# Input projection of a hybrid Fourier and attention step, twelve pairs of channel blocks by one level of Strassen's recursion

## The chip, the cores and the metric

One core of a Trainium2 chip runs the whole step. The metric is the device time of one execution in microseconds (us), median over runs. The engines run beside each other, each through its own instruction queue in order: TensorE (PE, matrix products; its weight loads are PEld), VectorE (DVE), ScalarE (ACT), GpSimd (POOL) and SyncE (SP, which issues DMA transfers; POOL and ACT issue some too). Waits between engines are semaphores.

## What is computed

One layer on 1024 latent and 128 context tokens of 1024 channels, in float32. Cut to what matters here:

```python
h = rms_norm(x) * (1 + scale) + shift
u_f, z_f, cq, ckv, k_rope, z_a, g_f, g_a = split(h @ w_in)   # 512 512 256 128 32 512 1024 1024
y_f = (fourier_mix(u_f) * silu(z_f)) @ w_f_out
y_a = (attention(cq, ckv, k_rope) * silu(z_a)) @ w_a_out
merged = sigmoid(g_f) * y_f + sigmoid(g_a) * y_a
x = x + gate * (merged @ w_out)                              # then a final norm
```

Fourier mixing is linear, so `u_f` is never formed: its weights are transformed and folded into the first part. What this change concerns is the rest of the input projection: `z_f`, `z_a`, `g_f`, `g_a` (3072 channels, 24 blocks of 128) and the low-rank part `cq, ckv, k_rope` (416 channels).

## The kernel before

Channels lie on the 128 partitions, tokens along the columns. Every float32 operand is kept as two parts, a high one rounded to PE's format and a low rest, and `mm3` makes one product from three matmuls: high by high, low by high, high by low. `hi_pool` rounds on POOL and `lo_dve` makes the rest on DVE; `split` does both for a loaded tile.

The first part loads tokens, normalises, transposes and modulates them into `hTh`/`hTl` (8 tiles of 128 channels x 1152 tokens, high and low), and mixes folded positions through the Fourier weights (order written out in `SEQ`). The mixing's last matmul starts at 89.14 us of the profiled span. Then, in the order of the program:

- Fourier gates: `load_in` brings a block of 128 channels of `w_in` (512 KB) and splits it; `proj(w, c)` multiplies it with one of three chunks of `CH` = 384 tokens, 8 tiles x 3 matmuls. `gated` applies ACT's sigmoid and DVE's product. Four blocks, `zf`.
- The position transform (matrices loaded by `load_r` on POOL's queue, products L125 to L129 on `dft` tiles and L566, L567), whose results are combined and multiplied with `zf` into `fz`.
- 8 blocks of `g_a` by `merge_gate`, stored to DRAM; 8 blocks of `g_f`, each with the Fourier output map (`w_f_out`, 12 matmuls a chunk) and DVE's product L679.
- The low-rank part: `low_mm` (9 token tiles x 24 matmuls of 416 columns, norms and rotation) and `low_tr` (transposes; per tile ACT copies and DVE differences), set between blocks of `merge_gate`.
- 4 blocks of `z_a` by `gated`, with the first keys, queries and values between them; then the attention, the output map with the merge, and the output projection, none of which the change edits.

That makes 72 chunks x 24 = 1728 matmuls of 128 x 384 by `proj`.

The engines' instruction orders come from a scheduler that reorders the program by estimates. SBUF tiles of up to 4.6 KB a partition come from one pool of `NU` = 40 buffers (`U`), PSUM from 8 banks (`MM`): a load or a product waits until a buffer's last reader is done.

Of the kernel before, what the change touches and what calls it, by code (L numbers as in the profile page):

```python
# [64 lines left out]
def kernel(ctx: ExitStack, tc: tile.TileContext, a: dict):  # L65
# [56 lines left out]
    tail = [None]  # L122

    def mm3(out, lh, ll, rh, rl, start, stop, after=False):
        i = pe.matmul(out, lh, rh, start=start, stop=False)  # L125
# [2 lines left out]
        pe.matmul(out, lh, rl, start=False, stop=False)  # L128
        tail[0] = pe.matmul(out, ll, rh, start=False, stop=stop)  # L129
# [318 lines left out]
    def load_in(i):
        return split_w(a["w_in"][i], [P, 8, P])

    def proj(w, c):
        wh, wl = w
        ps = MM()
        sl = slice(c * CH, (c + 1) * CH)
        for k in range(8):
            mm3(ps[:, :CH], wh[:, k, :], wl[:, k, :], hTh[k][:, sl], hTl[k][:, sl], k == 0, k == 7)
        return ps

    def gated(w, out, hook=None):
        for c in range(3):  # L460
            ps = proj(w, c)
            s = H([P, CH], s="sz")
            act.activation(s, ps[:, :CH], AF.Sigmoid)
            dve.tensor_tensor(out=out[:, c * CH : (c + 1) * CH], in0=ps[:, :CH], in1=s, op=ALU.mult)
            if hook:
                hook(c)

# [16 lines left out]
    pool.memset(zer, 0.0)
# [1 line left out]
    pool.memset(ex, 0.0)
# [49 lines left out]
    zf = []  # L536
    ahead = []
    for m in range(4):
        w = wn
        wn = load_in((1, 2, 3, 16)[m])  # L540
        if m == 3:
            ahead.append(load_in(17))
        z = U([P, NT], F32, "zf")
        gated(w, z)
        zf.append(z)
        if m == 0:
            freq512()
        if m == 2:
            ch, cl, sh, sl_ = [load_r(a["pos"][i], [P, 2, 512]) for i in range(4)]
# [31 lines left out]
    fz = []  # L581
    for p in range(2):
        qs = slice(p * P, (p + 1) * P)
        ss = slice(256 + p * P, 256 + (p + 1) * P)
# [6 lines left out]
        Ev, Fv = U([P, 640], F32, "E"), U([P, 640], F32, "F")
        dve.tensor_tensor(out=pairs(Ev[:, 0:512]), in0=pairs(A[:, 0:512]), in1=freqs(pb), op=ALU.subtract)
        dve.tensor_tensor(out=pairs(Fv[:, 0:512]), in0=pairs(A[:, 0:512]), in1=freqs(pb), op=ALU.add)
        dve.tensor_tensor(out=Ev[:, 512:640], in0=A[:, 512:640], in1=pc[:, 128:256], op=ALU.subtract)
        dve.tensor_tensor(out=Fv[:, 512:640], in0=A[:, 512:640], in1=pc[:, 128:256], op=ALU.add)
        for r in range(2):
            f = U([P, NT], F32, "f")
            z = zf[2 * p + r]
            if r == 0:
                x0, x1 = Ev, Fv  # L600
            else:
                x0, x1 = Fv, Ev
                for i in range(2):
                    g = 2 * p + i
                    act.copy(Fv[64 * i : 64 * i + 1, :], a64[32 * g : 32 * g + 1, :])
# [709 lines left out]
```

## Time and profile before

| | us |
|---|---|
| median of 3 runs | 957.46 |
| lowest and highest of them | 956.80, 958.73 |
| span of the profiled execution | 955.9 |
| first part, to the mixing's end: PE busy | 63.75 of 89.30 |
| projection, Fourier part, first keys (89.3 to 525): PE busy | 433.59 of 435.70 |
| attention (525 to 800): PE busy | 272.46 of 275.00 |
| output map, output projection (800 to the end): PE busy | 147.42 of 155.90 |

The page gives no time of its own for the profiled execution beside the span. Durations of single instructions below come from it. A row of a group reads: line, engine, operation, output<-inputs, shape, count | busy us in all, mean ns of one | idle us of the engine just before them, and what ended the idle time. A matmul's duration is its latency; several are under way at once.

### The profile page before, as it was taken

How to read it: one execution, taken by the hardware profiler on the slowest of the kernel's cores; microseconds unless marked ns; L12 is line 12 of the kernel's file. 1: busy time of each engine (PE TensorE's matmuls, PEld its weight loads, DVE VectorE, ACT ScalarE, POOL GpSimd, SP SyncE). 2: the span in 40 equal slices, each digit the busy share in tenths (PEclk: the TensorE clock that was granted, in tenths of full speed). 3: DMA queues.
4: the chain of work that ended last, by engine and by line, in shares of the span. 5: the costliest groups of instructions: out<-in, count | busy, mean ns of one | idle time of the engine just before them, and what ended most of it. 6: DMA issues, size and time to landing. Idle time of an engine off the chain costs nothing.

```text
span 955.9 us, 14669 instructions
## 1 busy us (share of the span) xinstructions
PE 917.2 (96%) x5550; PEld 870.5 (91%) x5550; DVE 527.9 (55%) x1141; ACT 381.8 (40%) x1050; POOL 291.2 (30%) x360
## 2 busy tenths in 40 slices
PE   4878999999999999999999999999999999999996
PEld 3668999999999999999999999999999989988885
DVE  3999324312211134332116888888888888883333
ACT  7565113200000103212125787787787783112111
POOL 1588203201000110000223146245245126773221
PEclk9999999999999999999999999999999999999999
DMA  9703401231314331113200000000000057443222
GB/s 363 287 1 109 133 1 31 76 111 64 146 58 170 117 103 47 34 40 119 89 1 6 10 1 7 10 1 9 8 1 7 1 183 274 138 154 111 88 89 89
DMA packets 25279, 78.49 MB, mean 82 GB/s; under 512 B 3316, under 2 KB 6004, under 8 KB 25208
## 3 DMA queue, kind: packets, MB, share of 16 engines
q1 hardware_dynamic: 23624, 74.59, 22.2%
q0 software_dynamic: 864, 2.49, 0.8%
q8 instruction: 44, 0.72, 0.3%
q10 hardware_dynamic: 720, 0.47, 0.2%
q14 instruction: 27, 0.22, 0.1%
HBM read 63.29 MB, written 14.25 MB: 81 GB/s over the span
## 4 chain that ended last, share of the span: by engine, by line
PE 87%; DVE 7%; ACT 2%; issue 1%; DMA 1%; POOL 0%; SPq 0%; DVEq 0%; ACTq 0%; POOLq 0%
PE mm L125 25%; PE mm L129 24%; PE mm L128 24%; PE mm L939 6%; PE mm L960 3%; PE mm L959 3%; DVE fo L220 1%; DVE tl L110 1%; DVE hf L295 1%; DVE fol L220 1%; DMA x<-in_x_prompt 1%; ACT junk L367 1%; DVE sd L220 1%; DVE hTl L220 1%; DVE wpl L110 1%
## 5 line engine op out<-in xcount | busy, mean ns | idle before, releaser
L129 PE MATMUL mm<-hTh,lo 128*128 128x384 f32 x576 | 194.1, 338 | 2.1 <-DVE lo L110 2.1
L125 PE MATMUL mm<-hTh,hi 128*128 128x384 f32 x576 | 194.9, 338 | 0.0
L128 PE MATMUL mm<-hTl,hi 128*128 128x384 f32 x576 | 194.1, 337 | 0.0
L107 POOL TENSOR_SCALAR hi<-wr 128x1024 fp32r<-128x1024 f32 (+2 forms) x37 | 44.0, 1192 | 269.1 <-DMA wr<-in_w_in 189.5
L907 DVE TENSOR_REDUCE s<-mm 128x1 f32<-128x384 f32 (+1 forms) x200 | 104.7, 539 | 15.6 <-PE mm L129 13.3
L918 ACT ACTIVATE p<-mm,s 128x384 f32<-128x384 f32 x192 | 110.3, 589 | 7.1 <-DVE s L912 6.9
L110 DVE TENSOR_TENSOR tl<-mm,th 128x384 fp32r<-128x384 f32 (+1 forms) x216 | 102.7, 504 | 16.9 <-ACT th L940 16.2
L125 PEld LDWEIGHTS mm<-hTh,hi 128*128 128x128 f32 x576 | 108.1, 188 | 3.5 <-issue 3.4
L129 PEld LDWEIGHTS mm<-hTh,lo 128*128 128x128 f32 x576 | 108.2, 188 | 2.4 <-DVE lo L110 2.4
L128 PEld LDWEIGHTS mm<-hTl,hi 128*128 128x128 f32 x576 | 108.1, 188 | 0.1
L940 ACT CAST th<-mm 128x384 fp32r<-128x384 f32 (+1 forms) x216 | 89.6, 461 | 25.2 <-PE mm L939 23.0
L939 PE MATMUL mm<-c,p 128*128 128x128 f32 x576 | 95.5, 274 | 1.6 <-ACT s L918 0.5
L679 DVE TENSOR_TENSOR mf<-mm,sgf 128x384 f32<-128x384 f32 x24 | 13.4, 557 | 131.1 <-PE mm L129 127.1
L939 PEld LDWEIGHTS mm<-c,p 128*128 128x128 f32 x576 | 71.7, 140 | 8.4 <-DVE tl L110 1.4
L960 PE MATMUL mm<-tl,v 128*128 128x384 f32 (+1 forms) x216 | 73.9, 346 | 0.2 <-DVE tl L110 0.2
L959 PE MATMUL mm<-th,v 128*128 128x384 f32 (+1 forms) x216 | 73.3, 343 | 0.0
L125 PE MATMUL mm<-kh,q 128*128 128x384 f32 x192 | 70.7, 368 | 0.7 <-DVE osb L973 0.4
L110 DVE TENSOR_TENSOR lo<-wr,hi 128x1024 fp32r<-128x1024 f32 (+2 forms) x37 | 50.0, 1356 | 29.9 <-POOL hi L107 28.8
L675 ACT ACTIVATE sgf<-mm 128x384 f32<-128x384 f32 x24 | 11.8, 492 | 135.7 <-PE mm L129 135.7
L128 PE MATMUL mm<-kl,q 128*128 128x384 f32 x192 | 64.8, 338 | 0.0
L129 PE MATMUL mm<-kh,q 128*128 128x384 f32 x192 | 63.8, 337 | 0.0
L125 PE MATMUL mm<-hi,mh 128*128 128x512 f32 (+1 forms) x152 | 57.7, 383 | 0.0
(314 smaller groups left out, 1965.7 us busy)
## 6 DMA issues: line engine op xcount, KB each, us to landing
wr<-in_w_in SPq DMA_DIRECT2D x24, 512.0 KB, 4.3
x<-in_x_sample SPq DMA_DIRECT2D x16, 512.0 KB, 5.6
wada<-in_w_ada SPq DMA_DIRECT2D x16, 512.0 KB, 10.1
ga_d<-ga SPq DMA_DIRECT2D x8, 576.0 KB, 3.2
mf_d<-mf SPq DMA_DIRECT2D x8, 576.0 KB, 3.2
gal<-ga_d SPq DMA_DIRECT2D x8, 576.0 KB, 3.7
mfl<-mf_d SPq DMA_DIRECT2D x8, 576.0 KB, 4.9
wgate<-in_w_gate SPq DMA_DIRECT2D x8, 512.0 KB, 7.5
```

Of the source, the lines that this page charges most:

```text
L107: pool.tensor_scalar(out=out, in0=x, scalar1=1.0, scalar2=1.0, op0=ALU.mult, op1=ALU.mult)
L110: dve.tensor_tensor(out=out, in0=x, in1=hi.bitcast(F32), op=ALU.subtract)
L125: i = pe.matmul(out, lh, rh, start=start, stop=False)
L128: pe.matmul(out, lh, rl, start=False, stop=False)
L129: tail[0] = pe.matmul(out, ll, rh, start=False, stop=stop)
L220: (pool if ENG[k] == "p" else dve).tensor_tensor(out=out, in0=x, in1=y, op=op)
L907: dve.tensor_reduce(out=self.nb if self.last else self.mx[:, kc : kc + 1], in_=ps[:, 0:n], axis=AX.X, op=ALU.min)
L918: act.activation(self.p[:, kc * CH : kc * CH + n], self.ps[kc][:, 0:n], AF.Exp, scale=-1.0, bias=self.nb, accum_out=SSP[(self.h // 2) % 2] ...
L939: pe.transpose(pt[:, j * P : (j + 1) * P], self.pr[j][:, kt * P : (kt + 1) * P], ident)
L940: act.copy(th[:, i, 0:n], pt[:, 0:n])
L959: pe.matmul(po[:, 0:n], V[kt][:, h, :], th[:, i, 0:n], start=(self.nv == 0), stop=False)
L960: pe.matmul(po[:, 0:n], V[kt][:, h, :], tl[:, i, 0:n], start=False, stop=(self.nv == 8))
```

## The change

The 24 blocks are taken as 12 pairs. For a pair, the weights are a 2 x 2 matrix (two channel blocks by two halves of the 1024 input channels) and the tokens another (two halves of the input channels by two halves of 576 tokens). Seven products of the half size, on sums and differences of these parts, take the place of eight (Winograd's form of Strassen's scheme):

- `combine(f)` (four times) adds high and low parts of two token tiles on POOL, makes the differences on DVE and POOL, and splits them again; `replace_b12` puts one difference in the place of a part that is no longer needed. That is possible only after the low-rank part has read the tokens, so `low_mm` moves to the front, its results go to DRAM (`low_d`), and `low_tr` reads them back after the pairs, without gate blocks between its tiles.
- `Blocks.prepare` makes the seven weight operands of the next pair while `pair` runs: 5 sums or differences and 7 roundings of 128 x 512 on POOL, 7 rests on DVE.
- `pair` runs 7 products x 2 x 4 x 3 = 168 matmuls of 288 columns; DVE adds what PSUM doesn't, ACT takes sigmoids, POOL multiplies.
- The Fourier part follows the first `low_mm` at once, its results go to DRAM (`f_d`) and are multiplied in the last two pairs; all gates (`ga_d`, `gf_d`, `za_d`) are stored and read back; the Fourier output map comes after the pairs by itself.
- `NU` grows from 40 to 43, a DMA scratch area shrinks for it, and all comments are gone (so line numbers move).

```diff
-NU = 40
-NF = 3
+NU = 43
...
-    for i, m in enumerate(range(NF, 8)):
-        w = wn
-        wn = load_in(17 + m if m < 7 else 4)
-        if i < 3:
-            low = low_mm(i)
-        merge_gate(w, m)
-        if i < 3:
-            low_tr(i, low)
...
+    def combine(f):
+        xa, xb = U([P, NT], F32, "xa"), U([P, NT], F32, "xb")
+        for x, k in ((xa, f), (xb, f + 4)):
+            pool.tensor_tensor(out=x, in0=hTh[k].bitcast(F32), in1=hTl[k].bitcast(F32), op=ALU.add)
+        x11, x12, x21, x22 = xa[:, lo_half], xa[:, hi_half], xb[:, lo_half], xb[:, hi_half]
+        dve.tensor_tensor(out=x11, in0=x12, in1=x11, op=ALU.subtract)
+        pool.tensor_tensor(out=x12, in0=x22, in1=x12, op=ALU.subtract)
+        dve.tensor_tensor(out=x22, in0=x22, in1=x11, op=ALU.subtract)
+        dve.tensor_tensor(out=x21, in0=x21, in1=x22, op=ALU.subtract)
+        h, l = U([P, NT], F32R, "th"), U([P, NT], F32R, "tl")
+        act.copy(h, xb)
+        lo_dve(l, xb, h)
+        t42.append((h, l))
...
+        act.copy(h, x12)
+        lo_dve(l, x12, h)
+        ones.append(x11)
+
+    def replace_b12(f):
+        h, l = hTh[f][:, hi_half], hTl[f][:, hi_half]
+        act.copy(h, ones[f])
+        lo_dve(l, ones[f], h)
...
+        def prepare(self, j):
+            (a11, a12), (a21, a22) = [(r[:, 0], r[:, 1]) for r in self.raw]
+            if j == 6:
+                self.s12 = U([P, 2, 512], F32, "ws")
+                pool.tensor_tensor(out=self.s12[:, 0], in0=a21, in1=a22, op=ALU.add)
+                pool.tensor_tensor(out=self.s12[:, 1], in0=self.s12[:, 0], in1=a11, op=ALU.subtract)
+            elif j == 7:
+                self.s34 = U([P, 2, 512], F32, "ws")
+                pool.tensor_tensor(out=self.s34[:, 0], in0=a11, in1=a21, op=ALU.subtract)
+            elif j == 3:
+                pool.tensor_tensor(out=self.s34[:, 1], in0=a12, in1=self.s12[:, 1], op=ALU.subtract)
+            x = {1: lambda: a11, 2: lambda: a12, 3: lambda: self.s34[:, 1], 4: lambda: a22, 5: lambda: self.s12[:, 0],
+                 6: lambda: self.s12[:, 1], 7: lambda: self.s34[:, 0]}[j]()
+            w = U([P, 2, 512], F32R, "wp")
+            hi_pool(w[:, 0], x)
+            lo_dve(w[:, 1], x, w[:, 0])
+            self.w[j] = w
...
+    def product(b, j, ps, n, first):
+
+        w = b.w[j]
+        for f in range(4):
+            ws = slice(f * P, (f + 1) * P)
+            rh, rl = moving(j, f, n)
+            mm3(ps[:, 0:NQ], w[:, 0, ws], w[:, 1, ws], rh, rl, first and f == 0, f == 3, on=True)
...
+    ORDER = (1, 6, 2, 7, 5, 4, 3)
...
+        for j in ORDER:
+            for n in range(2):
+                B = {1: X, 2: X, 6: Y, 7: Y, 4: Y, 5: Z, 3: Z}[j]
+                if j in (1, 6, 5):
+                    B[n] = MM()
+                product(b, j, B[n], n, j in (1, 6, 5))
+                ps, t = B[n][:, 0:NQ], tmp[n]
+                if j == 1:
+                    act.copy(t[:, 0], ps)
+                elif j == 6:
+                    dve.tensor_tensor(out=t[:, 1], in0=ps, in1=t[:, 0], op=ALU.add)
+                elif j == 2:
+                    done(0, 0, n, ps)
+                elif j == 7:
+                    dve.tensor_tensor(out=t[:, 2], in0=ps, in1=t[:, 0], op=ALU.add)
+                elif j == 5:
+                    done(1, 1, n, (ps, t[:, 2]))
+                elif j == 4:
+                    done(1, 0, n, (ps, t[:, 0]))
+                else:
+                    done(0, 1, n, (ps, t[:, 1]))
+            if nxt:
+                nxt.prepare(j)
...
+    PAIRS = [("g", ga_d, 16 + i, i) for i in (0, 2, 4, 6)] + [("g", gf_d, 8 + i, i) for i in (0, 2, 4, 6)]
+    PAIRS += [("z", za_d, 4, 0), ("z", za_d, 6, 2), ("f", None, 0, 0), ("f", None, 2, 2)]
...
+    freq512()
+    for p in range(2):
+        fourier_out(p)
+    combine(1)
+    low_mm(1)
+    combine(2)
+    nb_ = Blocks(PAIRS[0][2])
+    for j in ORDER:
+        nb_.prepare(j)
+    low_mm(2)
+    combine(3)
+    for f in range(4):
+        replace_b12(f)
...
+    lows = [(t, low_load(t)) for t in (9, 0, 1, 2, 3, 4, 5, 6, 7, 8)]
+    for t, row in lows:
+        low_tr(t, row)
```

Three places in the engines' orders. First POOL at the end of the mixing, before (`fol` is the mixing's last operand, `hi` a rounded weight tile, `cax` small constants, `zer`, `ex` and `c` tiles that are cleared):

```order
L220 TENSOR_TENSOR fol_866<-fo_846,foh_865 128x512
L107 TENSOR_SCALAR hi_967<-wr_965 128x1024
L480 DMA cax_971<-in_chan 128x512
L484 MEMSET zer_975 128x970
L516 DMA cax_971<-in_alt 128x256
```

and of the change, with `dft` the position matrices and `wr_985` a quarter of the low-rank weights:

```order
L217 TENSOR_TENSOR fol_866<-fo_846,foh_865 128x512
L460 DMA cax_971<-in_chan 128x512
L463 MEMSET c_195_974 128x970
L464 MEMSET ex_972 128x706
L445 DMA dft_977<-in_pos 128x1024
L445 DMA dft_979<-in_pos 128x1024
L445 DMA dft_981<-in_pos 128x1024
L445 DMA dft_983<-in_pos 128x1024
L582 DMA cax_971<-in_alt 128x256
L106 TENSOR_SCALAR hi_987<-wr_985 128x832
```

The rounding of the first weights stood right behind `fol`; now eight instructions stand between them.

Second, POOL during the last low-rank tiles of the change (`wp` weight operands of the first pair, `ws` their sums, `xa` and `xb` the sums of token tiles 3 and 7):

```order
L106 TENSOR_SCALAR wp_1555<-ws_1552 128x512
L106 TENSOR_SCALAR wp_1558<-wr_1545 128x512
L685 TENSOR_TENSOR ws_1561<-wr_1545,wr_1547 128x512
L687 TENSOR_TENSOR ws_1561<-wr_1545,ws_1552 128x512
L106 TENSOR_SCALAR wp_1563<-ws_1561 128x512
L106 TENSOR_SCALAR wp_1566<-ws_1552 128x512
L106 TENSOR_SCALAR wp_1569<-wr_1547 128x512
L106 TENSOR_SCALAR wp_1573<-ws_1561 128x512
L530 TENSOR_TENSOR xa_1715<-hTh_819,hTl_820 128x1152
L530 TENSOR_TENSOR xb_1716<-hTh_901,hTl_902 128x1152
```

where POOL had only this, at the Fourier gates before:

```order
L107 TENSOR_SCALAR hi_1039<-wr_1037 128x1024
L107 TENSOR_SCALAR cax_971<-ex_972 128x353
L107 TENSOR_SCALAR hi_1139<-wr_1137 128x1024
L107 TENSOR_SCALAR hi_1230<-wr_1228 128x1024
L471 DMA dft_1319<-in_pos 128x1024
```

The weights of the first pair and the sums of the last token tiles, both new, are now in one queue, the sums last.

Third, PE at the low-rank transposes (those with `c_72`, the identity), before:

```order
L129 MATMUL mm_3232<-hTh_901,lo_2881 128x384
L712 MATMUL mm_3259<-c_72,s_3145 128x128
L713 MATMUL mm_3259<-c_72,s_3147 64x128
L781 MATMUL mm_3268<-c_72,s_3143 128x128 x2
...
L712 MATMUL mm_3291<-c_72,s_3169 128x128
L713 MATMUL mm_3291<-c_72,s_3171 64x128
L781 MATMUL mm_3300<-c_72,s_3167 128x128 x2
L125 MATMUL mm_3314<-hi_2972,hTh_541 128x416
```

and of the change, from the last pair's last product to the output map (`whl`):

```order
L126 MATMUL mm_4449<-hTh_901,wp_4309 128x288
L858 MATMUL mm_4611<-c_72,low_4589 128x128
L859 MATMUL mm_4611<-c_72,low_4589 64x128
L858 MATMUL mm_4620<-c_72,low_4593 128x128
L859 MATMUL mm_4620<-c_72,low_4593 64x128
L888 MATMUL mm_4629<-c_72,low_4593 128x128 x2
...
L858 MATMUL mm_4748<-c_72,low_4609 128x128
L859 MATMUL mm_4748<-c_72,low_4609 64x128
L888 MATMUL mm_4757<-c_72,low_4609 128x128 x2
L122 MATMUL mm_4774<-hi_4530,whl_4584 128x384
```

Three tiles' transposes stood between blocks of other matmuls; now those of all ten tiles follow each other, and the map follows them.

More of the change, by code (lines that the diff above doesn't have):

```diff
@@ L437 @@
     hTh, hTl = [hTh[f] for f in range(8)], [hTl[f] for f in range(8)]
-    late = [None]
     def split_w(src, shape):
         raw = U(shape, F32, "wr")
-        dma = nc.sync.dma_start(raw, src)
-        late[0] = late[0] or dma
+        nc.sync.dma_start(raw, src)
         return split(raw)
[L448 to L466, printed above, removed]
     def load_r(src, shape):
@@ L482 @@
     C64 = U([P, 2, 5, 97], F32R, "c64")
-    zer = U([P, 2, 5, 97], F32, "zer")
-    pool.memset(zer, 0.0)
-    hi_pool(C64, zer)
+    pool.memset(C64.bitcast(F32), 0.0)
     pool.memset(ex, 0.0)
+    ch, cl, sh, sl_ = [load_r(a["pos"][i], [P, 2, 512]) for i in range(4)]
+    w4h, w4l = [], []
+    for q in range(4):
+        h, l = split_w(a["w416"][q], [P, 2, 416])
+        w4h.append(h)
+        w4l.append(l)
+    mid = U([P, 896], s="mid")
+    nc.sync.dma_start(mid[:, 0:512], a["mid"])
+    nc.sync.dma_start(mid[:, 512:768], a["q_norm_g"].to_broadcast([P, 256]))
@@ L534, in freq512 @@
         dve.tensor_scalar(out=col[0:97, 4:6], in0=pcol[0:97, 4:6], scalar1=float((NL * P) ** -0.5), scalar2=None, op0=ALU.mult)
-    zf = []
-    ahead = []
-    for m in range(4):
-        w = wn
[L540 to L549, printed above, removed]
+    low_mm(0)
+    combine(0)
     pas, pbs, p64 = [MM(), MM()], [MM(), MM()], MM()
@@ L588 @@
         A = U([P, 640], F32, "A")
-        act.copy(pairs(A[:, 0:512]), freqs(pa))
+        act.copy(pairs(A[:, 0:512]), freqs(pas[p]))
         act.copy(A[:, 512:640], pc[:, 0:128])
[L591 to L594, printed above, removed]
@@ L615, with fourier_out @@
-    mf_d = dram.tile([8, P, NT], F32, name="mf_d")
-    ga_d = dram.tile([8, P, NT], F32, name="ga_d")
+        pcs.append(pc)
+        As.append(A)
+    def fourier_out(p):
+        pb, pc, A = pbs[p], pcs[p], As[p]
+        f0, f1 = U([P, NT], F32, "f"), U([P, NT], F32, "f")
+        for f, o0, o1 in ((f0, ALU.subtract, ALU.add), (f1, ALU.add, ALU.subtract)):
+            dve.tensor_tensor(out=pairs(f[:, 1024:512:-1]), in0=pairs(A[:, 0:512]), in1=freqs(pb), op=o1)
+            dve.tensor_tensor(out=pairs(f[:, 0:512]), in0=pairs(A[:, 0:512]), in1=freqs(pb), op=o0)
+            dve.tensor_tensor(out=f[:, NL:NT], in0=A[:, 512:640], in1=pc[:, 128:256], op=o0)
+            act.copy(f[:, 512:513], col[:, 2 * p : 2 * p + 1])
+        nc.sync.dma_start(f_d[2 * p], f0)
+        for i in range(2):
+            g, rw = 32 * (2 * p + i), slice(64 * i, 64 * i + 1)
+            act.copy(f1[rw, 0:512], a64[g : g + 1, 0:512])
+            act.copy(f1[rw, 1023:512:-1], a64[g : g + 1, 1:512])
+            act.copy(f1[rw, NL:NT], a64[g : g + 1, 512:640])
+            act.copy(f1[rw, 512:513], col[g : g + 1, 4:5])
+        nc.sync.dma_start(f_d[2 * p + 1], f1)
@@ new lines, in moving @@
+    def moving(j, f, n):
+        o = n * NQ
+        if j == 1:
+            h, l = hTh[f], hTl[f]
+        elif j == 2:
+            h, l = hTh[f + 4], hTl[f + 4]
+        elif j == 3:
+            (h, l), o = (hTh[f + 4], hTl[f + 4]), o + NH2
+        elif j == 4:
+            h, l = t42[f]
+        elif j == 5:
+            (h, l), o = (hTh[f], hTl[f]), o + NH2
+        elif j == 6:
+            (h, l), o = t42[f], o + NH2
+        else:
+            (h, l), o = t33[f // 2], o + NH2 * (f % 2)
+        return h[:, o : o + NQ], l[:, o : o + NQ]
@@ new lines @@
+    PAIRS = [("g", ga_d, 16 + i, i) for i in (0, 2, 4, 6)] + [("g", gf_d, 8 + i, i) for i in (0, 2, 4, 6)]
+    PAIRS += [("z", za_d, 4, 0), ("z", za_d, 6, 2), ("f", None, 0, 0), ("f", None, 2, 2)]
+    fzs = []
+    freq512()
[11 more added lines that the diff above has]
+        replace_b12(f)
+    for i, (kind, dst, blk, m) in enumerate(PAIRS):
+        b = nb_
+        nb_ = Blocks(PAIRS[i + 1][2]) if i + 1 < len(PAIRS) else None
+        fs = None
+        if kind == "f":
+            fs = []
+            for e in range(2):
+                t = U([P, NT], F32, "fl")
+                nc.sync.dma_start(t, f_d[m + e])
+                fs.append(t)
+        pair(b, nb_, kind, dst, m, fs)
@@ L618, in load_half @@
+    hTh = hTl = t42 = t33 = ones = b = nb_ = None
+    fz = []
+    for f in fzs:
+        h, l = U([P, NT], F32R, "hi"), U([P, NT], F32R, "lo")
+        for c in range(3):
+            sl = slice(c * CH, (c + 1) * CH)
+            act.copy(h[:, sl], f[:, sl])
+            lo_dve(l[:, sl], f[:, sl], h[:, sl])
+        fz.append((h, l))
+    fzs = None
     def load_half(name, m):
@@ new lines, in low_tr @@
+    def low_tr(t, row):
+        sl = slice(t * P, (t + 1) * P)
+        ckn, kd = row[:, 256:384], row[:, 384:448]
+        if t == 9:
+            put_kv(ckn, kd, kvh[:, 1024:1152], kvl[:, 1024:1152], KB, slice(1024, 1152))
+            return
+        if t < 8:
+            put_kv(ckn, kd, kvh[:, sl], kvl[:, sl], KB, sl)
+        else:
+            put_kv(ckn, kd, kch, kcl, KC, slice(0, 128))
+        pt = MM()
+        for k in range(2):
+            pe.transpose(pt[:, k * P : (k + 1) * P], row[:, k * P : (k + 1) * P], ident)
+        for k in range(2):
+            act.copy(cqh[k][:, sl], pt[:, k * P : (k + 1) * P])
+            lo_dve(cql[k][:, sl], pt[:, k * P : (k + 1) * P], cqh[k][:, sl])
@@ L878 @@
-    hTh = hTl = None
+    for _ in range(3):
+        value_map(len(V))
     stage.close()
```

317 lines of the change are left out of this document (155 added, 162 removed).

## The prediction

> **What bounds the kernel now.** I read the page's busy time and chain first, then windows of the stage that the change rewrites.
>
> ```profile
> span 955.9 us, 14669 instructions
> PE 917.2 (96%) x5550; PEld 870.5 (91%) x5550; DVE 527.9 (55%) x1141; ACT 381.8 (40%) x1050; POOL 291.2 (30%) x360
> PE 87%; DVE 7%; ACT 2%; issue 1%; DMA 1%; POOL 0%; SPq 0%; DVEq 0%; ACTq 0%; POOLq 0%
> L129 PE MATMUL mm<-hTh,lo 128*128 128x384 f32 x576 | 194.1, 338 | 2.1 <-DVE lo L110 2.1
> ...
> L125 PE MATMUL mm<-hTh,hi 128*128 128x384 f32 x576 | 194.9, 338 | 0.0
> L128 PE MATMUL mm<-hTl,hi 128*128 128x384 f32 x576 | 194.1, 337 | 0.0
> ```
>
> TensorE (PE) is the chain. Three groups of 576 are the projection that the change replaces, 1728 matmuls of 384 columns. In all of it PE waited 2.1 us, once. The next rows (from:to, then busy us of PE, weight loads, DVE, ACT, POOL, then the granted clock) say what lies beside it.
>
> ```profile
> 100.00:150.00 50.00, 50.00 (x311) 49.99 (x310) 10.89 (x17) 5.41 (x11) 2.62 (x3) 1.00 0.18 63
> 150.00:300.00 150.00, 150.00 (x867) 147.82 (x865) 41.19 (x54) 21.46 (x45) 24.45 (x23) 1.00 0.29 101
> 300.00:525.00 225.00, 225.00 (x1269) 219.20 (x1269) 71.78 (x208) 50.26 (x155) 32.23 (x42) 1.00 0.18 62
> ```
>
> From 100 to 525 us PE is never idle, while DVE, ACT and POOL are busy a third of the time or less. So PE time removed here is span removed, and PE time that becomes a wait is span added.
>
> **What a matmul costs.** The 338 ns are latency; matmuls overlap. The price is the distance of starts (start, duration, engine, line).
>
> ```profile
> 122.49 0.49 ACT L463 ACTIVATE sz<-mm 128x384 f32<-128x384 f32 x1 [3.71 <-PE mm L129]
> ...
> 143.47 0.49 ACT L463 ACTIVATE sz<-mm 128x384 f32<-128x384 f32 x1 [3.70 <-PE mm L129]
> ```
> ```profile
> 148.84 0.28 PE L129 MATMUL mm<-dft,pq 128*128 128x256 f32 x1
> ...
> 150.25 0.28 PE L129 MATMUL mm<-dft,pq 128*128 128x256 f32 x1
> ```
>
> Each sigmoid ends a chunk of 24 matmuls; five chunks take 20.98 us, 0.175 us a matmul at 384 columns. Twelve steps at 256 columns take 1.41 us, 0.1175 each. A line through both (0.45 ns a column, 3 ns fixed) puts 288 columns, which the trace doesn't have, at 0.132 us. Bounds: 0.118 (the 256-column row) to 0.175 (the 384-column row); I take 0.132, since 256 is the nearer row and the line has almost no fixed part.
>
> Before: 72 chunks x 4.196 = 302 us. After: 12 pairs x 7 products x 2 halves x 12 = 2016 matmuls x 0.132 = 266 us. **Saved: 36 us.** By the bounds alone 64 saved to 51 lost.
>
> The Trainium skill ("TensorE: Matmul & The Clock Gate", section "Back-to-back issue gap") speaks against that: for streams of weight load and matmul it gives 81 ns at 128 columns and 131 ns at 512, a large fixed part, by which 2016 shorter matmuls would cost more than 1728 longer ones (an estimate from that section, on a line through its two figures: 205 us against 198); it is a rival below. The rows above don't agree: 175 ns already at 384, and nearly proportional to columns.
>
> **What a pair asks of the others.** A pair is 168 matmuls, 22.2 us of PE. Beside it:
>
> ```profile
> L107 POOL TENSOR_SCALAR whl<-wr 128x512 fp32r<-128x512 f32 x16 | 10.6, 660 | 7.8 <-DMA wr<-in_w_f_out 7.4 <-DMA wr<-in_w_a_out 0.4
> L608 POOL TENSOR_TENSOR f<-E,zf 128x512 f32<-128x512 f32 x2 | 2.6, 1295 | 35.8 <-DVE E L592 35.8
> L608 POOL TENSOR_TENSOR f<-F,zf 128x512 f32<-128x512 f32 x2 | 3.7, 1854 | 1.4 <-ACT F L605 1.4
> L110 DVE TENSOR_TENSOR whl<-wr,whl 128x512 fp32r<-128x512 f32 x16 | 15.2, 947 | 8.1 <-POOL whl L107 8.1
> L679 DVE TENSOR_TENSOR mf<-mm,sgf 128x384 f32<-128x384 f32 x24 | 13.4, 557 | 131.1 <-PE mm L129 127.1 <-PE mm L712 4.0
> L463 ACT ACTIVATE sz<-mm 128x384 f32<-128x384 f32 x24 | 11.8, 492 | 84.2 <-PE mm L129 80.7 <-POOL kl L113 3.4
> ```
>
> POOL makes the next pair's weights: 7 roundings x 0.66 + sums of 5 x 1.3 to 1.85 = 11 to 14 us. DVE: 7 x 0.95 + 10 evacuations of 288 columns at 557 x 288/384 = 0.42, 11 us. ACT: about 10 x 0.4 = 4 us. All fit in 22.2. Only the first Fourier pair goes over (14 POOL products of 288 columns at 0.73 to 1.04 on top, 21 to 29 us), and it has a pair of lead. A bank comes back at least 24 matmuls, 3.2 us, after its last use, against about 1 us of evacuation. So I cost the pairs' side work at nothing; PE hides it, up to 22.2 us a pair.
>
> **Start: mixing to first pair.** In the old kernel PE loses the 2.1 us above. The POOL order (shown with the change) now puts two memsets, the cosine and sine loads and the low-rank weights' rounding ahead of the first new matmul.
>
> ```profile
> 86.50 1.62 POOL L107 TENSOR_SCALAR hi<-wr 128x1024 fp32r<-128x1024 f32 x1
> 88.06 0.75 POOL L480 DMA_DIRECT2D cax<-in_chan  x1
> 88.82 0.92 POOL L484 MEMSET zer<- 128x970 f32 x1
> 91.41 0.68 POOL L486 MEMSET ex<- 128x706 f32 x1
> L471 POOL DMA_DIRECT2D dft<-in_pos x4 | 2.2, 548 | 4.5 <-PE mm L129 4.5
> L107 POOL TENSOR_SCALAR hi<-wr 128x832 fp32r<-128x832 f32 x4 | 3.6, 890 | 18.1 <-PE mm L129 11.2 <-DMA wr<-in_w 6.6
> ```
>
> From 86.5: 0.75 + 0.92 + 0.68 + 4 x 0.55 + 0.55 + 0.89 = 6.0, so 92.5 where PE's mixing is through at 89.26; with the low half behind, 3.5 us. After the Fourier sums, low-rank tiles wait for banks that ACT and DVE are still emptying: 1.4 (0 to 3, by two ACT copies of 0.5 and one DVE pass of 0.6 per bank).
>
> Then the real stall. POOL is in order; five roundings and two sums of block 0 wait for buffers that the last low-rank tile holds, and the sums of token tile 3 and 7 stand behind them. From the end of that tile: 5 x 0.66 + 2 x 1.3 = 5.9; two sums of 1152 columns at 1295/512 ns a column = 5.8; two DVE differences of 576 columns at 0.78 (half of the next row); a cast of 1.2. Together 14.5 us.
>
> ```profile
> L110 DVE TENSOR_TENSOR lo<-f,hi 128x1152 fp32r<-128x1152 f32 x4 | 6.3, 1565 | 5.6 <-POOL hi L107 5.6
> L107 POOL TENSOR_SCALAR hi<-f 128x1152 fp32r<-128x1152 f32 x4 | 4.6, 1154 | 4.9 <-DVE f L611 3.4 <-PE mm L129 1.5
> ```
>
> PE meanwhile has 60 matmuls that need no token tile 3 (24 of product 1, 18 each of 6 and 5), 7.9 us; product 2's ready ones are queued behind. It waits 6.4 us. Together 11.3, less the old 2.1: **+9** (4 to 14).
>
> **End: pairs to output map.** The low-rank transposes ran among gate products, each copy hidden. Now 40 stand bare.
>
> ```profile
> L718 DVE TENSOR_TENSOR kl<-mm,kh 64x128 fp32r<-64x128 f32 x18 | 4.8, 282 | 1.1 <-ACT kh L717 0.7
> L783 ACT CAST cqh<-mm 128x128 fp32r<-128x128 f32 x18 | 4.6, 276 | 0.1
> L110 DVE TENSOR_TENSOR cql<-mm,cqh 128x128 fp32r<-128x128 f32 x18 | 4.9, 284 | 0.2
> ...
> L781 PE MATMUL mm<-c,s 128*128 128x128 f32 x18 | 3.4, 273 | 0.0
> ```
> ```profile
> 525.75 0.60 PE L939 MATMUL mm<-c,p 128*128 128x128 f32 x4
> ```
>
> The last pair ends in a DVE sum, an ACT sigmoid, two POOL products and ACT's split of the Fourier rows, all ahead of the copies in their queues: about 4.3 us. The map's first matmul needs a bank that the 34th of 48 DVE differences frees: 34 x 0.28 = 9.5. So it starts 13.8 us after the pairs. The transposes fill little of that: four take 0.60 us with the last one's 0.27, 0.11 apart, 40 x 0.11 = 4.4. **+9.4** (4 to 11; 4 if DVE's share goes at half of these 0.28).
>
> **Smaller.** Seven value maps in a row and the first query's split stand bare before the attention: +1.5 (0 to 3; one DVE pass of 0.7 to two of each). The new stores and reloads are some 23 MB over 400 us where the DMA share is 0.18 to 0.29: nothing.
>
> **The clock.** What a gap does to PE's clock, by the last but two column:
>
> ```profile
> 36.00:39.00 3.00, 1.27 (x12) 0.65 (x12) 3.00 (x6) 3.00 (x7) 2.90 (x3) 1.00 0.69 276
> ...
> 40.00:43.30 3.30, 3.30 (x17) 3.27 (x16) 3.30 (x7) 3.05 (x4) 0.91 (x1) 0.50 0.02 5
> ```
>
> Three microseconds at 42% busy, and 3.3 at half clock follow; a matmul then takes twice as long. Two gaps of 6 to 9 us should each bring one: 2 x 1.65 = **+3.3** (0 to 5). [...]
>
> **Sum.** -36 + 9 + 9.4 + 1.5 + 3.3 = -12.8, span 943.1. The page gives no time for its own execution; the runs' median, 957.46, lies 1.6 over its span. Forecast: 944.7 us.
>
> **Rivals.**
> - *The gaps are filled.* POOL comes earlier and the transposes run at the engines' pitch: start +4, end +4, no clock loss: -36 + 4 + 4 + 1.5 = -26.5, about 931. For it: DVE and ACT are idle over half the stage. Against: the order of the queues.
> - *The gaps are wider.* POOL sums at 1854 per 512 (DVE beside it is busy), terms at their upper ends: -36 + 14 + 11 + 3 + 5 = -3, about 954.5.
> - *Each pair waits for its weights* (slower). Their buffers come free only when DVE, POOL and the stores are done with the pair before. It decides from 12.8/12 = 1.1 us a pair; at 2.3 us a pair, one POOL rounding and one sum late (0.66 + 1.6), the time is 944.7 + 28 = 973. Against: 11 to 14 us of POOL in 22.2.
> - *Shorter matmuls don't get shorter in step* (slower). It decides from (266 + 12.8)/2016 = 0.138 us a matmul; at 0.15, between the 256- and 384-column rows, 2016 cost the old 302 us: 944.7 + 36 = 981. For it: weight loads are busy 91% of the span. Against: twelve loads and matmuls at 0.1175 in the 256-column rows.
>
> **Chances.** Forecast (936 to 950) 0.55; filled 0.15; wider 0.14, of which 0.03 ends within 0.2% of 957.46, about what a measurement can tell from no change; weights late 0.10, of which 0.02 within it; no shorter 0.06. Faster 0.81, same 0.05, slower 0.14. The range 929 to 958 leaves out the slow cases and little below.
>
> **What would show it.** Right: rows of 288 columns starting 0.13 us apart; a pair every 22 us with PE at 100%; PE idle about 6 us just after the last low-rank tile, released by the ACT cast of th; about 9 us idle before the first map matmul, released by DVE cql; half clock right behind both. Wrong: PE waits for wp inside later pairs, or a pitch near 0.15.

## The result and the profile after

| | before | after |
|---|---|---|
| median of 4 runs each, us | 957.41 | 963.34 |
| lowest and highest | 956.80, 958.73 | 962.62, 964.67 |
| span of the profiled execution | 955.9 | 961.9 |
| mean granted clock of TensorE | 0.994 | 0.973 |

The ratio is 1.0063, with a 95% interval of 1.0049 to 1.0078: slower by 0.6%, where the forecast was 944.7 us and the range ended at 958. First the page of after: busy times, the chain, the clock in 40 slices, and two of the new groups.

```profile
span 961.9 us, 15881 instructions
PE 898.3 (93%) x5838; PEld 846.4 (88%) x5838; DVE 660.6 (69%) x1329; ACT 412.5 (43%) x1130; POOL 442.0 (46%) x511
PE 84%; DVE 9%; POOL 2%; ACT 2%; DMA 2%; issue 1%; DVEq 0%; POOLq 0%; ACTq 0%
PEclk9999997799999999997999999999999999999999
L126 PE MATMUL mm<-hTh,wp 128*128 128x288 f32 x384 | 116.6, 304 | 7.3 <-DVE wp L109 7.3
...
L122 PE MATMUL mm<-th,wp 128*128 128x288 f32 x288 | 85.4, 297 | 2.1 <-ACT th L537 2.1
```

DVE has 133 us more work, POOL 151 us more, and PE's busy time fell only by 19 us although the matmuls saved 35. The clock dips in the seventh and eighth slice (144 to 192 us) and the nineteenth. The windows of after put PE, weight loads, DVE, ACT and POOL beside each other, with the clock last but two:

```profile
120.00:130.00 10.00, 10.00 (x47) 9.78 (x47) 10.00 (x25) 6.49 (x18) 3.25 (x3) 0.83 0.19 72
130.00:140.00 10.00, 10.00 (x55) 9.90 (x53) 8.84 (x7) 4.82 (x17) 5.99 (x3) 1.00 0.80 290
140.00:150.00 10.00, 9.59 (x52) 9.27 (x50) 8.88 (x19) 5.65 (x17) 7.07 (x7) 1.00 0.12 50
150.00:160.00 10.00, 5.70 (x23) 5.44 (x24) 10.00 (x24) 0.00 (x0) 8.14 (x8) 0.66 0.21 77
160.00:170.00 10.00, 6.15 (x32) 5.60 (x32) 9.73 (x32) 0.13 (x2) 3.09 (x2) 0.77 0.00 1
170.00:180.00 10.00, 6.71 (x25) 5.67 (x25) 6.66 (x10) 4.52 (x8) 5.07 (x6) 0.50 0.60 196
180.00:190.00 10.00, 10.00 (x69) 10.00 (x69) 6.75 (x9) 1.27 (x3) 8.12 (x10) 0.87 0.01 2
300.00:310.00 10.00, 10.00 (x78) 10.00 (x76) 3.89 (x6) 2.58 (x6) 4.25 (x5) 1.00 0.60 224
...
440.00:450.00 10.00, 1.57 (x7) 1.25 (x8) 8.27 (x22) 6.08 (x25) 5.42 (x7) 0.60 1.03 407
```

Read it from the row at 300 us: there a pair runs as forecast, PE full, clock full, 0.1326 us from start to start. The loss lies at both ends of the pairs. From 150 to 190 us only 144 matmuls start (the four rows count 149, since a matmul that runs over a border stands in both rows), worth 144 x 0.1326 = 19.1 us: 20.9 of 40 us are lost, 11.4 to idle time (40 less 28.6 busy) and 9.5 to half clock, with the latency of the last matmul ahead of each gap. DVE, not PE, is the engine that is full or nearly full there, from 120 to 170 us. At 440 PE all but stands.

The four longest waits of PE after the change, from 89 to 470 us (what waits, for what: us in all, times, longest):

```profile
PE mm L888 <- DVE kl L864: 9.2, 2, 8.5
PE mm L126 <- DVE wp L109: 8.2, 3, 3.7
PE mm L122 <- POOL hi L106: 2.9, 1, 2.9
PE mm L122 <- ACT th L537: 2.1, 1, 2.1
```

Against the sum of the prediction, stage by stage (starts of the first and last matmul of each stage in both traces):

| us | forecast | measured |
|---|---|---|
| 2016 matmuls for 1728 | -36 | -34.8 (2016 x 0.1326 = 267.3 for 72 x 4.196 = 302.1) |
| mixing to the first pair, waits | +2.6 | +2.4 (4.5 less the old 2.1) |
| the same stretch, half clock | 0 | +3.5 |
| first pair: waits, with 0.4 before 150 us | +6.4 | +11.8 |
| pairs' stage: half clock and the rest | +1.65 | +9.8 |
| last pair to the output map, less 4.4 of transposes | +9.4, and 1.65 of clock | +12.4 |
| the remainder | +1.5, all before the attention | +0.9 |
| span | -12.8 | +6.0 |

Why the first pair is late shows in DVE's and POOL's rows of after (start, duration, engine, line). First DVE:

```profile
152.58 0.68 DVE L109 TENSOR_TENSOR wp<-wr,wp 128x512 fp32r<-128x512 f32 x1
...
156.69 3.12 DVE L109 TENSOR_TENSOR wp<-ws,wp 128x512 fp32r<-128x512 f32 x1
159.74 3.20 DVE L109 TENSOR_TENSOR wp<-wr,wp 128x512 fp32r<-128x512 f32 x1
162.86 0.26 DVE L145 TENSOR_SCALAR s<-s 128x6 f32<-128x6 f32 x1
...
169.49 0.34 DVE L501 SCALAR_TENSOR_TENSOR low<-mm,s,mid 128x128 f32<-128x128 f32 x1
169.75 0.28 DVE L512 TENSOR_TENSOR low<-s,s 128x32 f32<-128x32 f32 x2
169.95 0.75 DVE L532 TENSOR_TENSOR xa<-xa 128x576 f32<-128x576 f32 x1
...
174.40 0.74 DVE L535 TENSOR_TENSOR xb<-xb 128x576 f32<-128x576 f32 x1
```

POOL, and the cast on ACT, of the same stretch:

```profile
156.13 3.13 POOL L530 TENSOR_TENSOR xa<-hTh,hTl 128x1152 f32<-128x1152 f32 x1
159.22 3.16 POOL L530 TENSOR_TENSOR xb<-hTh,hTl 128x1152 f32<-128x1152 f32 x1
```
```profile
175.18 1.15 ACT L537 CAST th<-xb 128x1152 fp32r<-128x1152 f32 x1 [2.21 <-DVE xb L535]
```

POOL has the sums of token tiles 3 and 7 ready at 162.4 us, 13.5 after PE goes over from the low-rank part to the first pair (148.9); the forecast had 11.7. But the first difference of `combine(3)` starts at 169.95: between them in DVE's queue stand the root, the norms and the rotation of the last low-rank tiles (162.86 to 169.9) and four rests of weights. And while POOL adds, two rests of weights take 3.12 and 3.20 us on DVE, where the one at 152.58 took 0.68; each ends 0.55 us behind the POOL operation beside it. The cast that product 2 needs ends at 176.3, 27.4 us behind the low-rank part, where 14.5 were forecast. Yet only 2.1 us of PE's waits in the first pair are for that cast; 8.2 are for `wp`, the rests of the weights, which stand in the same queue of DVE. The sum of the prediction had no wait for them.

The Trainium skill ("SBUF — State Buffer", section "SBUF: two separate sides") has a rule for the 3.1 us: DVE and GpSimd share a pair of ports under an exclusive lock, held for a whole instruction, and a DVE operation with two SBUF inputs blocks against a GpSimd operation that reads SBUF. These rows agree: each of the two rests has two inputs and ends 0.55 us behind POOL's sum.

### The profile page after: what moved, and what is told of

It is laid out like the page before. It is cut to its first block, busy times and chain, and to the rows that moved or that the text cites. A ratio compares the mean times of both kernels' runs of the same rounds, so it can differ in the third digit from the quotient of the medians.

```text
span 961.9 us, 15881 instructions
## 1 busy us (share of the span) xinstructions
PE 898.3 (93%) x5838; PEld 846.4 (88%) x5838; DVE 660.6 (69%) x1329; ACT 412.5 (43%) x1130; POOL 442.0 (46%) x511
## 4 chain that ended last, share of the span: by engine, by line
PE 84%; DVE 9%; POOL 2%; ACT 2%; DMA 2%; issue 1%; DVEq 0%; POOLq 0%; ACTq 0%
PE mm L122 23%; PE mm L126 23%; PE mm L125 23%; PE mm L1066 6%; PE mm L1087 3%; PE mm L1086 3%; DVE fo L217 1%; DVE wp L109 1%; DVE tl L109 1%; DMA x<-in_x_sample 1%; DMA gfl<-gf_d 1%; ACT junk L364 1%; POOL mfl L1230 0%; DVE hf L292 0%; DVE sd L217 0%
## 5 line engine op out<-in xcount | busy, mean ns | idle before, releaser
L126 PE MATMUL mm<-hTh,wp 128*128 128x288 f32 x384 | 116.6, 304 | 7.3 <-DVE wp L109 7.3
L122 PE MATMUL mm<-hTh,wp 128*128 128x288 f32 x384 | 116.0, 303 | 0.9 <-ACT hTh L550 0.5
L125 PE MATMUL mm<-hTl,wp 128*128 128x288 f32 x384 | 116.2, 303 | 0.6 <-DVE hTl L109 0.6
L1034 DVE TENSOR_REDUCE s<-mm 128x1 f32<-128x384 f32 (+1 forms) x200 | 105.0, 541 | 15.5 <-PE mm L126 13.5
L122 PE MATMUL mm<-th,wp 128*128 128x288 f32 x288 | 85.4, 297 | 2.1 <-ACT th L537 2.1
L126 PE MATMUL mm<-th,wp 128*128 128x288 f32 x288 | 85.2, 296 | 1.0 <-DVE wp L109 1.0
L125 PE MATMUL mm<-tl,wp 128*128 128x288 f32 x288 | 85.3, 296 | 0.0
L126 PEld LDWEIGHTS mm<-hTh,wp 128*128 128x128 f32 x384 | 75.2, 196 | 7.7 <-DVE wp L109 7.7
L122 PEld LDWEIGHTS mm<-hTh,wp 128*128 128x128 f32 x384 | 74.9, 195 | 1.5 <-ACT hTh L550 0.9
L125 PEld LDWEIGHTS mm<-hTl,wp 128*128 128x128 f32 x384 | 75.0, 195 | 1.0 <-DVE hTl L109 1.0
L745 DVE TENSOR_TENSOR z<-mm,u 128x288 f32<-128x288 f32 x72 | 32.7, 455 | 49.8 <-PE mm L126 49.7
L106 POOL TENSOR_SCALAR q<-qf 128x384 fp32r<-128x384 f32 x24 | 12.3, 511 | 105.0 <-DVE qf L934 66.1
```

The source lines that it names most:

```text
L106: pool.tensor_scalar(out=out, in0=x, scalar1=1.0, scalar2=1.0, op0=ALU.mult, op1=ALU.mult)
L122: i = pe.matmul(out, lh, rh, start=start, stop=False, skip_group_check=on)
L125: pe.matmul(out, lh, rl, start=False, stop=False, skip_group_check=on)
L126: pe.matmul(out, ll, rh, start=False, stop=stop, skip_group_check=on)
L745: dve.tensor_tensor(out=outs[i][:, sl], in0=ps, in1=t, op=ALU.add)
L1034: dve.tensor_reduce(out=self.nb if self.last else self.mx[:, kc : kc + 1], in_=ps[:, 0:n], axis=AX.X, op=ALU.min)
```

## The experiments

The theory after this reading: at the first pair PE waits for DVE, which has the differences, rests, norms and roots in one queue and stands still beside POOL's sums; half clock follows; at the end the bare transposes and POOL's queue hold the map. Rivals: POOL's queue itself, as the prediction had it; or the clock, once it is down, is the root of the loss. Each run was made on one chip with the kernel before (957.72, 957.19, 956.91 and 957.36 us in the four groups of runs). The changed kernel was not run in these groups; a gain against it is taken from its median of 963.34.

**Transposes spread.** Eight of the ten tiles' transposes stand between the map's chunks:

```diff
-    for t, row in lows:
+    for t, row in lows[:2]:
         low_tr(t, row)
+    lows = lows[2:]
...
             dve.tensor_tensor(out=mf[:, sl], in0=ps[:, :CH], in1=gfl[:, sl], op=ALU.mult)
+            if lows:
+                low_tr(*lows.pop(0))
```

> The changed kernel with eight of the ten tiles' low-rank transposes set behind the first eight chunks of the Fourier output map, two ahead of it. In the changed kernel 16.8 us lie between the last pair's last matmul (437.84) and the map's first (454.61), of which 4.4 are the transposes. Theory (the copies stand bare): about 9 us come back, near 954. Rival (the copies only move the wait into the map, since ACT and DVE still have 48 each in order): under 3 us come back, 960 or more.

Measured 959.35 us (958.94 to 959.76), ratio 1.0014 (1.0005 to 1.0023): 4 us better, between the two expectations. The wait for `kl` went and another took most of its place, as PE's row shows:

```profile
444.37 0.69 PE L122 MATMUL mm<-hi,whl 128*128 128x384 f32 x1 [6.01 <-POOL whl L106]
```

The map's first weights stand on POOL behind the products of the Fourier rows, which the last pair makes last. The changed kernel has the same cause in front of its wait for `kl`: ACT's first copy of a transpose starts at 444.18, 6.3 us after PE is through with the pairs (437.84), behind the split of the Fourier rows, which waits for these products; the prediction had 4.3.

**First pair plain, weights loaded late.** The first pair's two blocks are made by eight products, as before the change, so that the preparation has 25 us of cover:

```diff
+    for i in range(2):
+        wh, wl = split_w(a["w_in"][PAIRS[0][2] + i], [P, 8, P])
+        gt = U([P, NT], F32, "z")
+        for c in range(3):
...
+                mm3(ps[:, :CH], wh[:, k, :], wl[:, k, :], hTh[k][:, sl], hTl[k][:, sl], k == 0, k == 7)
+            act.activation(gt[:, sl], ps[:, :CH], AF.Sigmoid)
...
     for i, (kind, dst, blk, m) in enumerate(PAIRS):
+        if i == 0:
+            continue
```

> The first pair of gate blocks by eight products as before (144 matmuls of 384 columns, 25.2 us, in place of 168 of 288, 22.2), so that the sums of the tokens and the first operands are made beside it. Theory (the loss is DVE's and POOL's preparation that stands bare in the first pair: 11.8 us of waits and about 8 of half clock after them): -20 + 3, near 946. Rival (the preparation takes SBUF buffers, and the plain pair's weights take them away, so the waits move to the second pair): 960 or more.

Measured 964.65 (ratio 1.0072, 1.0050 to 1.0094): no gain, the rival's number, but not for its reason. The cover itself came late, as PE and SP show:

```profile
162.79 0.69 PE L122 MATMUL mm<-hTh,hi 128*128 128x384 f32 x1 [11.37 <-DVE s L153]
```
```profile
155.25 2.35 SPq L518 DMA_DIRECT2D low_d<-low  x3
157.69 0.40 SPq L439 DMA_DIRECT2D wr<-in_w_in  x1
```

The load of its weights stood in SP's queue behind the stores of low-rank rows, and those wait for DVE's norms (until 155.25): the same full DVE, through SP. Behind it no pair waited for anything. So the edit was tried again with an earlier load (below).

**No sums on POOL.** ACT copies the high part in place of each POOL sum; the low parts of the summed tokens are left out.

```diff
-            pool.tensor_tensor(out=x, in0=hTh[k].bitcast(F32), in1=hTl[k].bitcast(F32), op=ALU.add)
+            act.copy(x, hTh[k].bitcast(F32))
```

> The eight sums of high and low part on POOL (1152 columns each) are replaced by ACT's copies of the high part: the low parts of the tokens are left out of the five products on sums. Six DVE operations that ran beside such a sum took 2.7 to 3.5 us in place of 0.7 to 1.0. Theory (DVE is held while POOL adds, and DVE's queue is what PE waits for): 10 to 15 us come back, 948 to 953. Rival of the prediction (POOL's own queue, the sums of the last tiles behind the roundings): only the last wait, 2 us, comes back: about 961. Rival clock: as the theory, if the gaps vanish.

Measured 957.21 (ratio 0.9984, 0.9972 to 0.9995): 6 us better, between the two. No difference and no rest of weights takes 3 us any more, the first pair's waits fall from 11.8 to 8.3 us, but DVE stays full from 140 to 170. The blocking is a part, not the whole.

**PE kept busy.** Two runs filled the idle time with matmuls that nobody reads, to hold the clock; the first with 84 of them and a PSUM bank of their own (the diff is the second's).

```diff
     def product(b, j, ps, n, first):
+        for i in range(left.pop((j, n), 0)):
+            tc.keep_in_program_order(pe.matmul((ps if j == 5 else spare[0])[:, 0:NQ], hTh[0][:, 0:P], hTh[4][:, 0:NQ], start=True, stop=True, skip_group_check=True))
```

> 84 matmuls of 288 columns that nobody reads stand ahead of the first pair's products, 26 where PE waits longest, so that PE is hardly idle there. Rival clock (the half clock of 22 us in the first pair is itself the loss): about 8 us come back, near 955. Theory (DVE's queue sets when the pair can go on, PE only waits longer where it was faster): 3 us or less come back, 960 to 964.

Measured 970.5 (ratio 1.0131, 1.0116 to 1.0146), outside both expectations: the bank was missed elsewhere (6.2 us of waits for one), so it decides little. The second, which shares banks with the products, had 100:

> 100 idle matmuls of 288 columns in the first pair, this time in a PSUM bank that the pair takes later anyway (the run before had one bank more in use, and PE waited 6.2 us for a bank). They keep PE busy 13 us of what was idle or at half clock. Rival clock (half clock, not the waits, is the loss): 8 us come back, near 955. Theory (DVE sets when the pair goes on): within 4 us of the changed kernel, 960 to 966.

Measured 975.85 (ratio 1.0191, 1.0174 to 1.0208), outside both expectations too, 12.5 us slower than the changed kernel; 100 fillers are 13.3 us of PE by themselves (100 x 0.1326, an estimate of what they cost). Thirty of them ran ahead of product 1 (149.0 to 153.1) and the clock stayed full until 161; yet the trace shows

```profile
160.14 3.19 DVE L109 TENSOR_TENSOR wp<-wr,wp 128x512 fp32r<-128x512 f32 x1
```
```profile
176.76 0.85 PE L122 MATMUL mm<-th,wp 128*128 128x288 f32 x2 [13.48 <-ACT th L537]
```

PE took the products in another order and waited for `th` in one piece, 13.5 us. The point is when `th` came: its cast ends at 176.7, as in the changed kernel (176.3), and DVE's rows stand some 0.4 us later than there, as they did ahead of the first pair. PE's speed in between did not move the cast: up to there DVE's chain sets the time, not the clock. What the half clock behind it costs, these two runs don't tell.

**First pair plain, weights early.** As above, but the two blocks are loaded and rounded before the last low-rank tiles.

```diff
+    raws = []
+    for i in range(2):
+        raws.append(U([P, 8, P], F32, "wr"))
+        nc.sync.dma_start(raws[i], a["w_in"][PAIRS[0][2] + i])
     combine(1)
     low_mm(1)
     combine(2)
-    nb_ = Blocks(PAIRS[0][2])
...
+    first = [split(r) for r in raws]
     low_mm(2)
     combine(3)
+    nb_ = Blocks(PAIRS[1][2])
```

> The first pair by eight products again, now with its two weight tiles loaded ahead of the low-rank rows' stores and rounded before the last low-rank tiles. Theory (the plain pair covers the preparation; in the run before, its weights' load stood on SP's queue behind stores that waited for DVE until 155.25): the 14 us of waits at 151 to 168 and the half clock after them go, -15 to -20 against that run, 945 to 950. Rival (DVE is so far behind that the plain pair's banks and rests wait for it all the same): 960 or more.

Measured **952.99** (951.48 to 954.49), ratio 0.9953 (0.9937 to 0.9968): 10.4 us better than the change, short of the 945 to 950 expected, but below both kernels, with 3 us more of matmuls in it (144 x 0.175 = 25.2 us for 168 x 0.1326 = 22.3). PE's three longest waits from 89 to 470 us:

```profile
PE mm L904 <- DVE kl L880: 8.7, 1, 8.7
PE mm L122 <- POOL hi L106: 2.9, 1, 2.9
PE mm L122 <- DVE u L759: 2.8, 1, 2.8
```

No wait for `wp` or `th` is left: PE has other work while the operands are made.

**A gate pair last** (with the transposes spread), so that the Fourier rows' products lie under a pair:

```diff
+    PAIRS = PAIRS[:7] + PAIRS[8:] + PAIRS[7:8]
```

> Transposes among the map's chunks as in the first run, and a gate pair last in place of a Fourier pair, so that no POOL products stand ahead of the map's weights. In the first run the map's first matmul waited 6.0 us for POOL's rounding of its weights, behind six products of the Fourier rows. Theory: that wait goes, 5 to 7 us and its half clock, 953 against 959.35. Rival (the wait goes over to DVE's copies of the transposes or to the weights' load): within 2 us of 959.

Measured 961.17 (ratio 1.0041, 1.0025 to 1.0056): no better than the spread transposes alone, as the rival had it. PE and SP of that run:

```profile
444.45 0.39 PE L860 MATMUL mm<-c,low 128*64 128x128 f32 x1 [5.44 <-DMA low<-in_cache_krope]
```
```profile
439.78 1.16 SPq L776 DMA_DIRECT2D gf_d<-z  x2
441.00 0.56 SPq L874 DMA_DIRECT2D low<-in_cache_krope  x1
441.66 4.96 SPq L870 DMA_DIRECT2D low<-low_d  x9
```

The wait for weights became one for loads: SP, in order, holds the last gates' stores until their sigmoid, with the low-rank rows' loads behind.

**DVE without norms.** The roots, norms and rotation of the low-rank rows are left out; ACT copies the rows.

```diff
-        rs = S([P, 6], tag="ms", bufs=4)
...
+            row = H([P, 448], s="low")
+            act.copy(row[:, 0:416], pss[j][:, 0:416])
+            act.copy(row[:, 416:448], pss[j][:, 384:416])
```

> The low-rank rows are copied by ACT as they are: roots, norms and rotation on DVE (and their results) are left out. Theory (DVE is behind by its work at the start, the norms of 27 rows' parts and three chains of roots being some 20 us of it): PE's waits for wp, hTl and th in the first pair fall from 11.8 us to under 4, and 12 us or more come back, 948 to 952. Rival (only the blocking by POOL's sums counts): the 6 us of that run are not reached, 958 or more.

Measured 955.10 (ratio 0.9979, 0.9966 to 0.9991): 8 us better, between the two. The waits of its first pair, in an execution that took 958.61:

```profile
PE mm L122 <- ACT hTh L533: 6.1, 1, 6.1
PE mm L122 <- ACT th L520: 5.8, 1, 5.8
```

All waits for `wp` are gone, which the norms in DVE's queue had made; what is left is the chain of the last sums, which POOL and DVE make one after the other (POOL is full from 150 to 170). So two chains end near each other, and taking one away leaves the other. The waits did not fall under 4 us, as expected: they are 11.9 us in two pieces, where the change has 11.8 in seven. What came back in this execution is mostly half clock: the pairs' stage takes 282.7 us for 267.2 of matmuls, so 3.6 us are lost beside the waits, where the change loses 9.8.

**Three runs that combine.** The first has the plain first pair and the spread transposes; the second only moves the token sums and POOL's differences to DVE; the third has all of it.

```diff
-            pool.tensor_tensor(out=x, in0=hTh[k].bitcast(F32), in1=hTl[k].bitcast(F32), op=ALU.add)
+            dve.tensor_tensor(out=x, in0=hTh[k].bitcast(F32), in1=hTl[k].bitcast(F32), op=ALU.add)
...
-        pool.tensor_tensor(out=x12, in0=x22, in1=x12, op=ALU.subtract)
+        dve.tensor_tensor(out=x12, in0=x22, in1=x12, op=ALU.subtract)
```

> First pair by eight plain products under which the operands of the second are prepared, and eight of the ten tiles' transposes set between chunks of the output map. Theory (two separate losses, one at the first pair, one behind the last): the gain of each adds up, 952.99 less the 4 us that the spread transposes brought alone, about 949 (946 to 951), with no wait for wp in any pair. Rival (behind the last pair the map waits for POOL's products of the Fourier rows whatever the transposes do): 952 to 954, with the wait for whl of 6 us.

Measured 948.68 (946.71 to 950.27), ratio 0.9910 (0.9897 to 0.9922). The gains add up, 10.4 and 4, though the rival's wait for `whl` (6.0 us) is there as well.

> The eight sums of high and low parts and the four differences that POOL made are made by DVE, all else as in the changed kernel. Theory (DVE's time is what the first pair waits for): DVE gets 8 operations of 1152 columns at some 1.3 us and 4 of 576 at 0.75 more, 13 us, and loses the some 14 us in which it stood still beside POOL's sums; the 576-column differences take 0.75 us in place of 3.1 to 3.2, and the time stays, 961 to 965. Rival (POOL's queue, with sums behind the roundings, is what the first pair waits for, as the prediction had it): the cast of th comes some 6 us earlier and the time is 955 to 958.

Measured 960.58 (959.91 to 962.78), ratio 1.0038 (1.0026 to 1.0051): 2.8 us better than the change, a gain barely clear of the noise (the change's interval begins at 1.0049), just below the theory's span and above the rival's. DVE and ACT of that run:

```profile
158.30 1.35 DVE L530 TENSOR_TENSOR xa<-hTh,hTl 128x1152 f32<-128x1152 f32 x1
159.56 1.35 DVE L530 TENSOR_TENSOR xb<-hTh,hTl 128x1152 f32<-128x1152 f32 x1
```
```profile
171.16 1.15 ACT L537 CAST th<-xb 128x1152 fp32r<-128x1152 f32 x1 [0.39 <-DVE xb L535]
```

DVE, already full, does the two sums in 2.6 us where POOL took 6.3 with DVE blocked beside it, and the cast comes 4 us earlier.

> The kernel with both edits, and the token sums on DVE in place of POOL. Theory: with plain products ahead of the first pair neither engine's preparation is waited for, so the place of the sums changes nothing, within 1.5 us of the kernel with both edits. Rival (DVE is still at its limit there): 3 us or more slower, with waits for wp back in the first pair.

Measured **944.25** (942.22 to 944.76), ratio 0.9857 (0.9842 to 0.9872). Neither expectation: 4.4 us better than without the moved sums, where 1.5 at most was expected. In the traces the first matmul of the pairs comes 0.8 us earlier and their stage is 3.5 us shorter, with a wait for `u` of 1.0 us where 2.6 stood and no half clock in it up to 200 us: DVE's time still counted behind the plain pair.

**All, with a gate pair last and its stores on ACT's queue.**

```diff
-                nc.sync.dma_start(dst[m + i], outs[i])
+                (nc.sync if nxt else nc.scalar).dma_start(dst[m + i], outs[i])
```

> First pair plain, transposes spread, token sums on DVE, and a gate pair as the last of the pairs, whose two stores are issued by ACT and not ahead of the low-rank rows' loads on SP. Theory (what is left behind the pairs is the wait for the products and the split of the Fourier rows, which now lie under the last pair): the 6.0 us wait for whl goes and with it some half clock, 944.25 less 5 to 8, 936 to 940. Rival (as in the run with a gate pair last, the loads of the low-rank rows still come late): a wait of 3 us or more for low at the first transposes, 942 to 946.

Measured 943.41 (939.71 to 945.49), ratio 0.9859 (0.9842 to 0.9875): not told apart from the run before it, and in the rival's span, though its wait for `low` isn't there. In the profiled execution (939.71, the fastest) the map's first matmul stands at 419.27, right behind the first transposes, but PE waits further on; PE and SP there:

```profile
432.22 0.44 PE L122 MATMUL mm<-hi,whl 128*128 128x384 f32 x1 [3.97 <-POOL whl L106]
```
```profile
412.98 11.66 SPq L886 DMA_DIRECT2D low<-low_d  x9
424.74 0.38 SPq L982 DMA_DIRECT2D tab<-in_tab  x1
425.21 0.38 SPq L838 DMA_DIRECT2D wr<-in_w_f_out  x1
```

The wait is for the second block's weights, whose load is issued only at 425.21, behind the nine loads of low-rank rows. That another order of the loads would gain more was not tried.

## Why the prediction was wrong, point by point

- **What a matmul costs: right.** 0.1326 us at 288 columns against 0.132, -34.8 against -36. The rival of matmuls that don't shrink falls. The two figures of the Trainium skill ("TensorE: Matmul & The Clock Gate", section "Back-to-back issue gap") don't hold here: 288 columns already take longer than the 131 ns that it gives for 512.
- **The pairs' own side work at nothing: right** from the second pair to the end; the windows there have PE at 10.00. The rival of weights late in each pair falls.
- **Start: the step that failed.** "Together 14.5 us": it counted five roundings and four sums on POOL, then "two DVE differences of 576 columns at 0.78" and a cast, as if DVE were free. POOL's part was right within 2 us (POOL itself waited 1.9 us for DVE). But the low-rank part, moved to the front, brings its norms and roots to just this place, and the same queue has the rests of the weights and of the sums; the view of DVE busy a third of the time was taken from before, where nothing of that stood there. It measured 27.4 us to the cast, and the first pair's waits 11.8 us in place of 6.4, of which 8.2 are for the rests of the weights (`wp`), a wait that the sum put at nothing. (By its own terms, 14.5 less 7.9, the sum should have had 6.6.) The runs bear out DVE's queue: removing norms alone (8 us), sums on POOL alone (6) or moving them (2.8, barely clear of noise) each helped, and covering all with plain products helped most (10.4).
- **POOL beside DVE: missed.** The rival of wider gaps used a slower POOL sum "(DVE beside it is busy)", 1854 ns; that DVE itself would stand still, 3.1 us for 0.7, was not in it. Some six DVE operations were blocked this way between 93 and 163 us, by about 2.4 us each.
- **The clock: mechanism right, size wrong.** "Two gaps of 6 to 9 us should each bring one" stretch of half clock: the first pair had gaps one behind another and stayed at half clock for most of 153 to 183, over 9 us lost there, and two stretches ahead of the pairs came on top (3.5). How the wait is cut up counts: without the norms, 11.9 us in two pieces cost 3.6. Half clock is a consequence: in the run with both edits and the sums on DVE, which has one wait of 1.0 us there, the clock is 1.00 in every window from 140 to 200 us.
- **End: mechanism right, size 12.4 for 11.** DVE's `kl` was the late one, about 9 us, where DVE's `cql` was named, and the pair's own tail took 6.3 us for 4.3. That spreading the transposes recovers only 4 of it, since POOL's products and weights end there too, and then the loads, was not foreseen.
- **Smaller: a small sum right by luck.** The +1.5 before the attention isn't in the trace. The 0.9 is a remainder: the mixing ends 0.6 us earlier, and the attention and what follows take 1.5 us more, of which the prediction had nothing and whose cause is open.

Of the 19 us that separate forecast and result, the first pair holds 13.6, the clock ahead of it 3.5, the end 1.4 and the matmuls 1.2; the small terms take back the rest.

## What to carry to other kernels

When a rewrite buys TensorE time with additions on other engines, cost each of those engines at the place where the new work is due, in queue order with what else was moved there, not by its share of the old span. A new pipeline needs cover for its first operands: leaving the first unit in the old form cost 3 us of matmuls and won 10. In these runs, sums of two SBUF operands on POOL were no free help for a DVE that does the same.
